# Four modulations of the second layer computed on VectorE, and a longer weight window

## The chip, the core and the metric

The kernel runs on one core of one Trainium2 chip. The metric is the device time of one execution in microseconds (us), as a median over runs. The engines of the core are TensorE (PE: matrix products), VectorE (DVE), ScalarE (ACT), GpSimd (POOL) and SyncE (SP), which here only issues transfers from HBM.

## What is computed

Two stacked blocks work on 256 tokens of width 1024. The first block has two layers, each of this form; the second block (a scan, two attentions, three gated branches) is not touched.

```python
c_act = jax.nn.silu(c)
for l in range(DEPTH):
    mod = c_act @ w_ada[l] + b_ada[l]
    sh1, sc1, g1, sh2, sc2, g2 = [t[:, None, :] for t in jnp.split(mod, N_ADA, axis=-1)]
    h = rmsnorm(x, norm_mix_g[l]) * (1.0 + sc1) + sh1
    z = h @ w_in[l]
    ...
    x = x + g1 * (o @ w_out[l])
    h = rmsnorm(x, norm_mlp_g[l]) * (1.0 + sc2) + sh2
    x = x + g2 * (jnp.square(jax.nn.relu(h @ w_up[l])) @ w_down[l])
```

`mod` does not depend on x. Below, modulation (l, s) is chunk s of layer l: s = 0 to 5 stand for sh1, sc1, g1, sh2, sc2, g2. Each is a product of one row of 1024 with a 1024x1024 matrix.

## The kernel before

**Weights.** Every fp32 weight arrives in tiles `w` of 128x1024 (512 KB), in the order of one list, `e.stream`. `next_w` (L295) asks for the next `AHEAD_W` entries of the list and splits the next `AHEAD_S`. A split tile becomes a high part `wh` (a cast on ScalarE, L290) and a low part `wl` = w - wh (VectorE, L292), and TensorE takes three matmuls for each block of it: high by high, low by high, high by low (`mm`, L318). All tiles share 8 buffers `w` (`NW`) and 4 pairs `wh`, `wl` (`NS`), so a transfer on SP's queue waits until a buffer is read for the last time. Tiles of `w_ada` are used whole, without a split.

**A modulation on TensorE.** `ada_step` multiplies each of the 8 tiles of a modulation with a stationary operand of 32 equal columns (`ca32`, the activated c), 4 blocks a tile, as fp32: the trace counts 64 matmul records for one modulation. `ada_end` copies the sums to SBUF on ScalarE (L515, a buffer of the tag `pt1`, of which there are 2), turns them with 2 small matmuls (`adat`) and adds the bias on VectorE (L520, `mod`).

**A modulation on GpSimd.** `ada_pool` multiplies each tile with a column of c (`tensor_scalar`, L531) and adds it to a running tile of 128x1024 (`tensor_tensor`, L533). `ada_rows` then sums that tile over its partitions on TensorE with ones (4 blocks, 8 records), and `ada_end` follows.

**A norm.** ScalarE squares x in 4 pieces (L406, tag `pt1`), VectorE folds them (L393, L399), TensorE sums over partitions (`st`), VectorE and GpSimd form the inverse root (`rv` L375, `rsy` L358), TensorE spreads it (`bc`), and then for each of 8 chunks VectorE makes `nt` (L551), ScalarE `ah` (L552) and VectorE `al` (L553). The wide products `g` read `ah` and `al`.

**The MLP.** For g = 0 to 15 the product with w_up of group g gives `g`, its squared relu is split into `uh`, `ul` (L970, L971), and one step later the product with w_down of group g is added to four `acc` banks. At the end x += g2 * acc (L1029). Layer 0's MLP is followed by the layer boundary: the norm of layer 1 and its first product, w_in1.

**Where layer 1's modulations stand.** (1,0) and (1,1) on GpSimd during layer 0's MLP (`ad_mlp`), (1,2) and (1,3) on TensorE at the layer boundary (`ad_next`), (1,4) on TensorE at layer 1's second norm (`ad_norm`), (1,5) on GpSimd during layer 1's MLP. Pieces of work wait in one queue, `e.q`; `fill` takes the oldest piece and `need(tag)` empties the queue up to the last piece of a tag. A scheduler then sets each engine's final order from data dependences and priorities; the splits and norms have a raised priority.

## Time and profile before

| | |
|---|---|
| three runs | 1837.41, 1836.98 and 1834.9 us, median 1836.98 us |
| profiled execution | 1838.83 us, of which 1837.0 us are the span |
| mean granted TensorE clock | 0.992 of full speed |
| busy over the span | PE 98%, DVE 73%, ACT 55%, POOL 20% |
| transfers | 346.88 MB, mean 189 GB/s |

Busy means that an instruction runs on the engine; the span is the stretch from the first to the last instruction. Idle time of an engine is noted with what ended it, which is an inference from semaphores.

### The profile page before, as it was taken

What the parts mean: (1) busy time and instruction counts of PE and PEld (TensorE: products, weight loads), DVE (VectorE), ACT (ScalarE), POOL (GpSimd) and SP (SyncE); (2) the same over time, 40 slices, a digit from 0 to 9 for tenths busy, and PEclk for the clock granted to TensorE, in tenths of its full rate; (3) what the DMA queues carried; (4) which work ended last, traced back from release to release, by engine and by line L of the source; (5) the groups of instructions that cost most, each with busy time, mean ns of one, the idle gap of its engine ahead of it and who ended that gap; (6) DMA issues with size and microseconds to landing.
All of it is one profiled execution on the core that took longest, in us unless ns stands there. A gap on an engine that the chain in (4) does not pass through costs nothing.

```text
span 1837.0 us, 37186 instructions
## 1 busy us (share of the span) xinstructions
PE 1791.6 (98%) x14800; PEld 1696.7 (92%) x14800; DVE 1334.8 (73%) x2212; ACT 1017.1 (55%) x1882; POOL 358.9 (20%) x291
## 2 busy tenths in 40 slices
PE   7999999999998999999999999999999999999998
PEld 6878799987878999999999999999999999999998
DVE  4575775756778655798897897566687897997566
ACT  4354444444545444557777575454556687675552
POOL 0000271800007300002444202200001445202200
PEclk9999999999998999999999999999999999999999
DMA  9873886757447655554444644465553445554451
GB/s 335 317 246 129 301 272 197 258 197 294 130 138 282 230 182 183 168 171 140 143 162 154 191 161 148 166 205 175 193 175 130 148 160 162 181 166 168 153 183 60
DMA packets 98223, 346.88 MB, mean 189 GB/s; under 512 B 12288, under 2 KB 13440, under 8 KB 97792
## 3 DMA queue, kind: packets, MB, share of 16 engines
q1 hardware_dynamic: 98048, 344.50, 55.5%
q8 instruction: 116, 1.90, 0.4%
q14 instruction: 59, 0.48, 0.1%
HBM read 339.01 MB, written 1.05 MB: 185 GB/s over the span
## 4 chain that ended last, share of the span: by engine, by line
PE 90%; DVE 3%; ACT 2%; DMA 2%; issue 1%; POOL 0%; POOLq 0%; SPq 0%; DVEq 0%; ACTq 0%
PE g L318 68%; PE acc L318 10%; PE yps L318 2%; DVE wl L292 1%; PE sc L318 1%; PE ada L318 1%; PE ds L318 1%; PE o L318 1%; DMA w<-w_ada 1%; ACT wh L290 1%; PE do L318 1%; PE xs L318 1%; PE xo L318 1%; DMA w<-w_up 1%; PE tw L1153 1%
## 5 line engine op out<-in xcount | busy, mean ns | idle before, releaser
L292 DVE TENSOR_TENSOR wl<-w,wh 128x1024 fp32r<-128x1024 f32 x518 | 664.3, 1285 | 337.7 <-ACT wh L290 335.5
L290 ACT CAST wh<-w 128x1024 fp32r<-128x1024 f32 x518 | 540.6, 1047 | 510.9 <-PE g L318 328.3
L318 PE MATMUL g<-xh,wh 128*128 128x256 f32 x1664 | 477.1, 287 | 0.7 <-DVE cv L1234 0.4
L318 PE MATMUL g<-xl,wh 128*128 128x256 f32 x1664 | 472.3, 284 | 0.0
L318 PE MATMUL g<-xh,wl 128*128 128x256 f32 x1664 | 471.7, 284 | 0.0
L318 PEld LDWEIGHTS g<-xh,wh 128*128 128x128 f32 x1664 | 319.3, 192 | 13.0 <-issue 6.9
L318 PEld LDWEIGHTS g<-xl,wh 128*128 128x128 f32 x1664 | 319.4, 192 | 0.8 <-issue 0.7
L318 PEld LDWEIGHTS g<-xh,wl 128*128 128x128 f32 x1664 | 319.4, 192 | 0.1
L318 PE MATMUL g<-ah,wh 128*128 128x256 f32 x736 | 210.4, 288 | 4.2 <-ACT ah L552 4.2
L318 PE MATMUL g<-al,wh 128*128 128x256 f32 x736 | 210.6, 287 | 2.5 <-DVE al L553 2.5
L318 PE MATMUL g<-ah,wl 128*128 128x256 f32 x736 | 210.8, 287 | 0.7 <-DVE wl L292 0.7
L358 POOL TENSOR_TENSOR rsy<-rv,mhalf 128x2 f32<-128x2 f32 (+1 forms) x14 | 13.4, 958 | 938.8 <-DVE rv L375 831.1
L318 PE MATMUL acc<-pt,wh 128*128 128x256 f32 x1024 | 183.1, 280 | 0.0
L1452 POOL PARTITION_BROADCAST E<-rows x64 | 96.6, 1571 | 389.0 <-PE tw L1153 157.7
L1451 ACT ACTIVATE E<-E,ltok 128x128 f32<-128x128 f32 x384 | 124.5, 394 | 61.9 <-POOL E L1452 57.9
L318 PEld LDWEIGHTS acc<-pt,wh 128*128 128x128 f32 x1024 | 156.8, 188 | 0.4 <-issue 0.4
L318 PEld LDWEIGHTS g<-ah,wh 128*128 128x128 f32 x736 | 142.2, 194 | 8.0 <-ACT ah L552 4.4
L318 PEld LDWEIGHTS g<-al,wh 128*128 128x128 f32 x736 | 142.7, 194 | 4.5 <-DVE al L553 3.5
L318 PEld LDWEIGHTS g<-ah,wl 128*128 128x128 f32 x736 | 142.6, 194 | 1.3 <-DVE wl L292 1.1
L318 PE MATMUL acc<-pt,wl 128*128 128x256 f32 x512 | 142.3, 279 | 0.0
L531 POOL TENSOR_SCALAR sb<-w,ca 128x1024 f32<-128x1024 f32 x24 | 89.3, 3721 | 62.6 <-PE ada L318 32.8
L318 PEld LDWEIGHTS acc<-pt,wl 128*128 128x128 f32 x512 | 96.2, 188 | 0.0
(384 smaller groups left out, 3571.4 us busy)
## 6 DMA issues: line engine op xcount, KB each, us to landing
w<-w_ada SPq DMA_DIRECT2D x96, 512.0 KB
w<-w_up SPq DMA_DIRECT2D x64, 512.0 KB
w<-w_down SPq DMA_DIRECT2D x64, 512.0 KB
w<-w_br SPq DMA_DIRECT2D x64, 512.0 KB
w<-w_gl SPq DMA_DIRECT2D x48, 512.0 KB
w<-w_in SPq DMA_DIRECT2D x36, 512.0 KB
w<-w_mem SPq DMA_DIRECT2D x32, 512.0 KB
w<-w_out SPq DMA_DIRECT2D x32, 512.0 KB
```

The lines of the kernel that those rows point to most:

```text
L290: nc.scalar.copy(wh, w)
L292: nc.vector.tensor_tensor(wl, w, wh.bitcast(F32), ALU.subtract)
L318: self.nc.tensor.matmul(o, l, r, start=start, stop=stop)
L358: self.nc.gpsimd.tensor_tensor(y, v, self.mhalf[:, 0:cols], ALU.pow)
L531: nc.gpsimd.tensor_scalar(dst, w, ca[:, 2 * n + i : 2 * n + i + 1], None, ALU.mult)
L1153: nc.tensor.transpose(tps[:, kt * S + t * P : kt * S + (t + 1) * P], src[:, t, kt * P : (kt + 1) * P], e.ident)
L1451: ex = lambda o, s, r: nc.scalar.activation(o, o, AF.Exp, bias=bias[:, s, r : r + 1])
L1452: nc.gpsimd.partition_broadcast(E, state["rows"][32 * (h % 4) : 32 * (h % 4) + 1, :])
```

## The change

Modulations (1,0) to (1,3) are computed by VectorE during layer 0's MLP (`ada_vec`): the first tile by a `tensor_scalar`, each of the next seven by a `scalar_tensor_tensor` that multiplies and adds to the running sum. Two modulations share one buffer `rows` of 128x2048 taken from a pool that exists already. The key of number j (of 16, two tiles each) is placed at g = 1 + 7j // 8. After the last tile, `ada_rows` is put at the end of the queue. (1,4) alone stays on TensorE at the boundary, (1,5) goes to TensorE at layer 1's second norm, and GpSimd has no modulation. `AHEAD_W` is 12 instead of 8, with 8 buffers as before; whole tiles count as ready as soon as they are asked for. In the list of tiles, w_up of group 1 stands ahead of the modulation of the second norm, and the second tile pair of w_in1 of layer 1 ahead of that of the boundary.

```diff
@@ -204,7 +204,8 @@
 
 
 NW, NS = 8, 4
-AHEAD_W, AHEAD_S = 8, 4
+AHEAD_S = 4
+AHEAD_W = NW + AHEAD_S
 SPLIT_FIRST, NORM_FIRST = 100, 200
 NU = 11
 ALPHA = (2 * DEPTH) ** 0.25
@@ -279,10 +280,13 @@
             ent[2] = self.t(self.wp, [P, 1024], "w", bufs=NW)
             self.last_dma = self.nc.sync.dma_start(ent[2], ap[:, i * 1024 : (i + 1) * 1024])
 
+    def _whole(self, ent):
+        return ent[0][0].startswith(("w_ada", "cmp_"))
+
     def _split(self, ent):
         nc = self.nc
         key, _, w, _ = ent
-        if key[0].startswith(("w_ada", "cmp_")):
+        if self._whole(ent):
             ent[3] = w
             return
         with self.tc.high_priority(offset=SPLIT_FIRST):
@@ -295,7 +299,7 @@
     def next_w(self, *key):
         for i, ent in enumerate(self.wq[:AHEAD_W]):
             self._fetch(ent)
-            if i < AHEAD_S and ent[3] is None:
+            if ent[3] is None and (i < AHEAD_S or self._whole(ent)):
                 self._split(ent)
         i = next(i for i, ent in enumerate(self.wq) if ent[0] == key)
         assert self.wq[i][3] is not None, key
@@ -458,10 +462,16 @@
 
     ad_early = lambda l: ada(l, 2) if l == 0 else []
     ad_mix = lambda l: ada(l, 3) + ada(l, 4) if l == 0 else []
-    ad_norm = lambda l: ada(l,5) if l == 0 else ada(l,4)
-    ad_mlp = lambda l: [(1,0),(1,1)] if l == 0 else [(1,5)]
-    ad_next = lambda l: ada(l+1,2)+ada(l+1,3)
-    mlp_keys = lambda l: {1 + 6 * i + n: [("w_ada", *p, n)] for i, p in enumerate(ad_mlp(l)) for n in range(4)}
+    ad_norm = lambda l: ada(l, 5)
+    ad_mlp = lambda l: [k for s in range(4) for k in ada(1, s)] if l == 0 else []
+    ad_next = lambda l: ada(l + 1, 4)
+
+    def mlp_keys(l):
+        out = {}
+        for j, key in enumerate(ad_mlp(l)):
+            out.setdefault(1 + 7 * j // 8, []).append(key)
+        return out
+
     MEM = 6
     a0 = ada(0, 0) + ada(0, 1)
     start = [[], a0[0:2], a0[2:4], a0[4:6], a0[6:8], []]
@@ -470,16 +480,17 @@
     for l in range(DEPTH):
         W = lambda i: ("w_in1", l, zorder[i])
         ea, am = ad_early(l), ad_mix(l)
-        e.stream(*([] if l else [W(0)]), W(1), W(2), *ea[0:2], ("cmp_k1", l), W(3), *ea[2:3], ("cmp_v1", l), W(4), *ea[3:4], W(5))
+        e.stream(*([] if l else [W(0), W(1)]), W(2), *ea[0:2], ("cmp_k1", l), W(3), *ea[2:3], ("cmp_v1", l), W(4), *ea[3:4], W(5))
         e.stream(W(6), *am[0:2], ("w_out1", l, 0), *am[2:3], W(7), ("w_out1", l, 1), *am[3:4], W(8), *am[4:])
-        e.stream(("w_out1", l, 2), ("w_out1", l, 3), ("w_up", l, 0), *ad_norm(l))
+        e.stream(("w_out1", l, 2), ("w_out1", l, 3), ("w_up", l, 0), ("w_up", l, 1), *ad_norm(l))
         nxt = mlp_keys(l)
         for g in range(16):
+            if g > 1:
+                e.stream(("w_up", l, g))
             if g >= 1:
-                e.stream(("w_up", l, g))
                 e.stream(("w_down", l, g - 1))
             e.stream(*nxt.get(g, []))
-        e.stream(("w_down", l, 15), *([("w_in1", l + 1, zorder[0])] if l + 1 < DEPTH else []), *ad_next(l))
+        e.stream(("w_down", l, 15), *([("w_in1", l + 1, zorder[i]) for i in range(2)] if l + 1 < DEPTH else []), *ad_next(l))
     e.stream(*[("w2_mem", 0, k) for k in range(MEM, 8)])
 
 
@@ -519,18 +530,21 @@
             v = lambda tl, i0: tl[:, i0 : i0 + 8].rearrange("p (j c) -> p c j", j=4)
             nc.vector.tensor_tensor(v(mods[l], s * 8), v3(tp[:, 0:8], 2), v(b_ada, l * 48 + s * 8), ALU.add)
 
-    def ada_pool(l, s, n):
+    def ada_vec(l, s, n):
 
         if n == 0:
-            boxes[l, s] = e.t(ap_, [P, 1536], "sb", bufs=2)[:, 0:D]
+            if s % 2 == 0:
+                boxes["rows"] = e.unit("rows")
+            boxes[l, s] = boxes["rows"][:, s % 2 * D : (s % 2 + 1) * D]
         rows = boxes[l, s]
         for i in range(2):
-            w = e.next_w("w_ada", l, s, n)
-            first = n == 0 and i == 0
-            dst = rows if first else e.t(ap_, [P, 1536], "sb", bufs=2)[:, 0:D]
-            nc.gpsimd.tensor_scalar(dst, w, ca[:, 2 * n + i : 2 * n + i + 1], None, ALU.mult)
-            if not first:
-                nc.gpsimd.tensor_tensor(rows, rows, dst, ALU.add)
+            w, c = e.next_w("w_ada", l, s, n), ca[:, 2 * n + i : 2 * n + i + 1]
+            if n == 0 and i == 0:
+                nc.vector.tensor_scalar(rows, w, c, None, ALU.mult)
+            else:
+                nc.vector.scalar_tensor_tensor(rows, w, c, rows, ALU.mult, ALU.add)
+        if n == 3:
+            e.add("mlp", lambda: ada_rows(l, s))
 
     def ada_rows(l, s):
         ps = e.gbank("ada")
@@ -539,7 +553,7 @@
 
     def ada_add(tag, keys):
         for key in keys:
-            e.add(tag, lambda key=key: (ada_pool if tag == "mlp" else ada_step)(*key[1:]))
+            e.add(tag, lambda key=key: (ada_vec if tag == "mlp" else ada_step)(*key[1:]))
 
     def norm_stats(src):
         return e.rms_wide(ap_, src, 1e-6)
@@ -1020,9 +1034,6 @@
             if g == 16:
                 e.add("mlp", lambda: down_last(15))
             ada_add("mlp", steps.get(g, []))
-            for i, p in enumerate(ad_mlp(l)):
-                if g == 6 * i + 8:
-                    e.add("mlp", lambda p=p: ada_rows(*p))
         e.need("mlp")
         ada_add("next", ad_next(l))
         for k in range(KC):
```

Three places in the engines' orders follow. In the rows of the changed kernel the line numbers are its own: L296 is `wl`, L526 the copy and L531 the `mod` of `ada_end`, L543 and L545 the operations of `ada_vec`, L565 to L567 the norm's `nt`, `ah`, `al`.

**VectorE at the second norm of layer 0.** `wl` of 128x1024 is the low part of w_up, group 1. Before:

```order
L292 TENSOR_TENSOR wl_2369<-w_2343,wh_2367 128x1024
L551 SCALAR_TENSOR_TENSOR nt_2385<-x_370,A_415_2383,bc_2321 128x256
L551 SCALAR_TENSOR_TENSOR nt_2389<-x_370,A_415_2383,bc_2321 128x256
L292 TENSOR_TENSOR wl_2424<-w_2349,wh_2422 128x1024
L520 TENSOR_TENSOR mod_13_105<-adat_2379,pack_1_70 128x2x4
L553 SCALAR_TENSOR_TENSOR al_2300<-nt_2385,mod_13_105,ah_2299 128x256
L553 SCALAR_TENSOR_TENSOR al_2300<-nt_2389,mod_13_105,ah_2299 128x256
L551 SCALAR_TENSOR_TENSOR nt_2393<-x_370,A_415_2383,bc_2321 128x256
L551 SCALAR_TENSOR_TENSOR nt_2397<-x_370,A_415_2383,bc_2321 128x256
L553 SCALAR_TENSOR_TENSOR al_2300<-nt_2393,mod_13_105,ah_2299 128x256
L553 SCALAR_TENSOR_TENSOR al_2300<-nt_2397,mod_13_105,ah_2299 128x256
```

After, from the fourth `nt` of the same norm on (`rows` is the running sum of modulation (1,0)):

```order
L565 SCALAR_TENSOR_TENSOR nt_2409<-x_378,A_421_2395,bc_2333 128x256
L543 TENSOR_SCALAR rows_2611<-w_2359,ca_98 128x1024
L567 SCALAR_TENSOR_TENSOR al_2312<-nt_2405,mod_13_105,ah_2311 128x256
L567 SCALAR_TENSOR_TENSOR al_2312<-nt_2409,mod_13_105,ah_2311 128x256
L565 SCALAR_TENSOR_TENSOR nt_2413<-x_378,A_421_2395,bc_2333 128x256
L545 SCALAR_TENSOR_TENSOR rows_2611<-w_2365,ca_98,rows_2611 128x1024
L565 SCALAR_TENSOR_TENSOR nt_2417<-x_378,A_421_2395,bc_2333 128x256
L567 SCALAR_TENSOR_TENSOR al_2312<-nt_2413,mod_13_105,ah_2311 128x256
L545 SCALAR_TENSOR_TENSOR rows_2611<-w_2371,ca_98,rows_2611 128x1024
L565 SCALAR_TENSOR_TENSOR nt_2421<-x_378,A_421_2395,bc_2333 128x256
L567 SCALAR_TENSOR_TENSOR al_2312<-nt_2417,mod_13_105,ah_2311 128x256
L545 SCALAR_TENSOR_TENSOR rows_2611<-w_2377,ca_98,rows_2611 128x1024
```

The two `wl` have moved ahead of the norm, to its first `fold` operations, and four of the new operations stand between `nt` and `al`.

**TensorE and ScalarE at the layer boundary.** TensorE before, where `ada_4584` is modulation (1,2) and `ada_4639` is (1,3):

```order
L318 MATMUL ada_4584<-w_4597,ca_11_101 32x256 x4
L318 MATMUL ada_4639<-w_4603,ca_11_101 32x256 x4
L318 MATMUL st_4574<-ones_72,fold_4565 128x1 x2
L318 MATMUL ada_4639<-w_4609,ca_11_101 32x256 x4
L318 MATMUL bc_4581<-pack_1_70,rsy_4579 128x128 x2
L318 MATMUL adat_4635<-pack_1_70,pt_725_4633 128x4 x2
L318 MATMUL ada_4639<-w_4615,ca_11_101 32x256 x4
L318 MATMUL ada_4639<-w_4621,ca_11_101 32x256 x4
L318 MATMUL g_4749<-ah_4559,wh_4463 128x256
```

TensorE after, from the end of layer 0's MLP on; `ada` read from `rows` are the sums of (1,0) to (1,3), `ada_4638` is (1,4):

```order
L322 MATMUL ada_4559<-rows_2611,ones_12_103 32x256 x3
L322 MATMUL ada_4570<-rows_2611,ones_12_103 32x256 x4
L322 MATMUL ada_4581<-rows_3549,ones_12_103 32x256 x4
L322 MATMUL adat_4566<-pack_1_70,pt_707_4564 128x4 x2
L322 MATMUL ada_4592<-rows_3549,ones_12_103 32x256 x4
L322 MATMUL adat_4577<-pack_1_70,pt_710_4575 128x4 x2
L322 MATMUL ada_4638<-w_4369,ca_11_101 32x256 x4
L322 MATMUL ada_4638<-w_4377,ca_11_101 32x256 x4
L322 MATMUL ada_4638<-w_4407,ca_11_101 32x256 x3
L322 MATMUL adat_4588<-pack_1_70,pt_713_4586 128x4 x2
L322 MATMUL ada_4638<-w_4407,ca_11_101 32x256
```

ScalarE before, where L406 are the squares of the norm:

```order
L290 CAST wh_4493<-w_4371 128x1024
L406 ACTIVATE pt_707_4561<-x_370 128x512
L406 ACTIVATE pt_708_4563<-x_370 128x512
L406 ACTIVATE pt_710_4567<-x_370 128x512
L406 ACTIVATE pt_711_4570<-x_370 128x512
L515 COPY pt_725_4633<-ada_4584 128x256
L552 ACTIVATE ah_4559<-nt_4698,mod_14_106 128x256
```

ScalarE after, where L410 are the same squares:

```order
L294 CAST wh_4511<-w_4332 128x1024
L294 CAST wh_4639<-w_4362 128x1024
L526 COPY pt_707_4564<-ada_4559 128x256
L526 COPY pt_710_4575<-ada_4570 128x256
L526 COPY pt_713_4586<-ada_4581 128x256
L526 COPY pt_716_4597<-ada_4592 128x256
L410 ACTIVATE pt_721_4615<-x_378 128x512
L410 ACTIVATE pt_722_4617<-x_378 128x512
```

One modulation has left TensorE here, the sums of all four have come, and four copies and one more pair of casts stand ahead of the squares.

**VectorE at the second norm of layer 1.** Before, the two `wl` belong to w_up of group 1, and `A` is computed from the modulation that TensorE does here:

```order
L399 TENSOR_TENSOR fold_6190<-fold_6190 128x256
L292 TENSOR_TENSOR wl_6254<-w_6228,wh_6252 128x1024
L375 TENSOR_SCALAR rv_6202<-st_6199 128x2
L292 TENSOR_TENSOR wl_6309<-w_6234,wh_6307 128x1024
L520 TENSOR_TENSOR mod_14_106<-adat_6264,pack_1_70 128x2x4
L958 SCALAR_TENSOR_TENSOR A_1015_6268<-mod_14_106,pack_1_70 128x8
L551 SCALAR_TENSOR_TENSOR nt_6270<-x_370,A_1015_6268,bc_6206 128x256
L551 SCALAR_TENSOR_TENSOR nt_6274<-x_370,A_1015_6268,bc_6206 128x256
```

After:

```order
L963 SCALAR_TENSOR_TENSOR x_378<-g_6168,mod_14_106,x_378 128x256 x2
L296 TENSOR_TENSOR wl_6211<-w_5807,wh_6209 128x1024
L397 TENSOR_TENSOR fold_6189<-fold_6189,pt_999_6191 128x512
L397 TENSOR_TENSOR fold_6189<-fold_6189,pt_1000_6194 128x512
L403 TENSOR_TENSOR fold_6189<-fold_6189 128x256
L379 TENSOR_SCALAR rv_6201<-st_6198 128x2
L565 SCALAR_TENSOR_TENSOR nt_6269<-x_378,A_1018_6267,bc_6205 128x256
L565 SCALAR_TENSOR_TENSOR nt_6273<-x_378,A_1018_6267,bc_6205 128x256
L531 TENSOR_TENSOR mod_14_106<-adat_6263,pack_1_70 128x2x4
```

Both `wl` are ahead of the norm's last folds, and `A` is no longer in this stretch; it is computed at the boundary.

## Rows read from the trace of the kernel before

**Rows 1.** Stretches: length, busy of PE, PEld, DVE, ACT, POOL; PEclk, DMA share, GB/s.

```profile
203.00:241.30 38.30, 34.48 (x293) 31.97 (x292) 28.83 (x41) 17.67 (x27) 24.12 (x9) 0.91 0.78 276
241.30:404.00 162.70, 162.70 (x1370) 160.98 (x1368) 106.36 (x94) 75.41 (x88) 72.63 (x23) 1.00 0.67 224
404.00:431.00 27.00, 24.19 (x249) 18.00 (x247) 15.37 (x31) 10.14 (x18) 0.72 (x1) 1.00 0.95 357
431.00:546.10 115.10, 109.94 (x895) 95.45 (x894) 82.61 (x254) 57.28 (x142) 2.34 (x2) 0.99 0.46 154
546.10:582.00 35.90, 28.04 (x247) 25.98 (x246) 28.07 (x37) 17.28 (x25) 21.03 (x8) 0.86 0.77 271
582.00:746.00 164.00, 164.00 (x1384) 163.45 (x1383) 100.58 (x95) 76.78 (x88) 28.59 (x9) 1.00 0.61 205
746.00:1837.00 1091.00, 1079.90 (x8764) 1042.79 (x8762) 854.92 (x1353) 674.19 (x1310) 206.24 (x234) 1.00 0.49 161
sum 1837.00, PE 1791.63 PEld 1696.71 DVE 1334.81 ACT 1017.09 POOL 358.89; mean PE 223.95 PEld 212.09 DVE 166.85 ACT 127.14 POOL 44.86
```

**Rows 2.** Timeline of PE: start, duration, [idle before, what ended it]; second norm, layer 0.

```profile
205.63 3.66 PE L318 MATMUL ada<-w,ca 128*32 128x256 f32 x64
210.93 0.71 PE L318 MATMUL bc<-pack,rsy 128*128 128x128 f32 x4 [1.10 <-POOL rsy L358]
213.79 0.50 PE L318 MATMUL g<-ah,wh 128*128 128x256 f32 x2 [1.31 <-ACT ah L552]
```

**Rows 3.** Timeline of DVE, the same place.

```profile
212.72 0.87 DVE L551 SCALAR_TENSOR_TENSOR nt<-x,A,bc 128x256 f32<-128x256 f32 x2
216.56 1.62 DVE L553 SCALAR_TENSOR_TENSOR al<-nt,mod,ah 128x256 fp32r<-128x256 f32 x2 [0.19 <-ACT ah L552]
221.86 0.89 DVE L553 SCALAR_TENSOR_TENSOR al<-nt,mod,ah 128x256 fp32r<-128x256 f32 x2 [0.18 <-ACT ah L552]
```

**Rows 4.** Line L1182: duration ns min/median/max of a 128x1024 operation on two tensors.

```profile
L1182 DVE SCALAR_TENSOR_TENSOR r<-r,mv,gb x2: 1274/1275/1276, 1826.0 to 1831.0; 128x1024 f32<-128x1024 f32 x2
```

**Rows 5.** Timeline of PE in layer 0's MLP: sums of one modulation, and its turn.

```profile
385.06 0.64 PE L318 MATMUL ada<-sb,ones 128*32 128x256 f32 x8
388.83 0.50 PE L318 MATMUL adat<-pack,pt 128*128 128x4 f32 x4
```

**Rows 6.** Timelines of PE and DVE at the layer boundary.

```profile
404.06 3.65 PE L318 MATMUL ada<-w,ca 128*32 128x256 f32 x62
414.14 0.39 PE L318 MATMUL g<-ah,wh 128*128 128x256 f32 x1
420.90 0.64 PE L318 MATMUL ada<-w,ca 128*32 128x256 f32 x8
411.83 0.87 DVE L551 SCALAR_TENSOR_TENSOR nt<-x,A,bc 128x256 f32<-128x256 f32 x2 [1.60 <-PE bc L318]
430.78 0.69 DVE L687 COPY z<-g 128x512 f32<-128x512 f32 x1 [2.46 <-PE g L318]
```

**Rows 7.** Timeline of PE, second norm of layer 1.

```profile
546.15 3.66 PE L318 MATMUL ada<-w,ca 128*32 128x256 f32 x64
554.39 1.22 PE L318 MATMUL bc<-pack,rsy 128*128 128x128 f32 x4 [4.04 <-POOL rsy L358]
559.15 0.80 PE L318 MATMUL g<-ah,wh 128*128 128x256 f32 x2 [2.90 <-ACT ah L552]
```

**Rows 8.** Timelines of ACT, DVE and POOL, the same place.

```profile
551.18 1.04 ACT L290 CAST wh<-w 128x1024 fp32r<-128x1024 f32 x1 [3.14 <-DMA w<-w_up]
552.26 1.23 DVE L292 TENSOR_TENSOR wl<-w,wh 128x1024 fp32r<-128x1024 f32 x1 [3.03 <-ACT wh L290]
556.54 1.23 DVE L292 TENSOR_TENSOR wl<-w,wh 128x1024 fp32r<-128x1024 f32 x1 [2.98 <-ACT wh L290]
565.48 3.01 DVE L553 SCALAR_TENSOR_TENSOR al<-nt,mod,ah 128x256 fp32r<-128x256 f32 x2 [0.18 <-ACT ah L552]
565.65 2.56 POOL L533 TENSOR_TENSOR sb<-sb,sb 128x1024 f32<-128x1024 f32 x1
```

## The prediction

> **What bounds the kernel now.** I read the stretches first [rows 1]. TensorE is busy 1791.63 of 1837.0 us, so nothing that only relieves another engine helps unless TensorE was waiting for it. In the two MLPs (241.3 to 404, 582 to 746) TensorE is busy in all of the 162.70 and 164.00 us: 1370 matmuls in 162.70 us are one each 0.119 us. There a wide matmul is the price of everything, and VectorE (106.36 us) has slack. The idle time that this change can reach lies in three short stretches: the second norm of layer 0 (34.48 busy of 38.30), the layer boundary (24.19 of 27.00) and the second norm of layer 1 (28.04 of 35.90). In the two norms the granted clock is also below 1 (0.91 and 0.86), meaning that for part of the stretch it stood at the lower of its levels, 1.2 instead of 2.4 GHz; the shortfall is worth 0.09 x 38.3 = 3.4 us and 0.14 x 35.9 = 5.0 us. At the boundary it is 1.00. Block 2 (746 to the end) keeps its instructions in the same order.
>
> Next I asked the timelines who is late there. In layer 1's second norm TensorE waits 4.04 us for the inverse root (bc <- rsy) and 2.90 us for the first ah [rows 7]. Neither is slow in itself: VectorE stood at `wl` of the next w_up tile for 3.03 and then 2.98 us, because ScalarE's cast waited 3.14 us for that tile's transfer [rows 8]. The root and the first nt are queued behind those two `wl`. Layer 0 has the same norm with waits of 1.10 and 1.31 us [rows 2]. Beside GpSimd's modulation an `al` pair takes 3.01 and 1.62 us where 0.89 is normal [rows 3, 8].
>
> **The change, part by part.** Terms are against the profiled execution, 1838.83 us.
>
> (a) *Second norm of layer 1.* The w_up tiles of group 1 now stand ahead of the 8 modulation tiles in SP's queue, so their `wl` come before the folds and nothing of the norm is behind a transfer. The modulation made here is (1,5), used only at the end of the MLP, so nt needs no fresh `A`. GpSimd is silent. The like-for-like model is layer 0: first wide product 213.79 - 205.63 = 8.2 us after the modulation's start [rows 2]. From there the 168 wide matmuls of this stretch take 168 x 0.119 = 20.0 us, together 28.2 us, and 31.6 us if the clock falls as in layer 0 (3.4 us). Before it is 582.0 - 546.15 = 35.85 us. So -7.7 to -4.3. The dear bound is layer 0 as it is: 241.3 - 205.63 = 35.7 us for 192, less 24 x 0.119 = 32.8 us, or -3.0. TensorE still idles before the first product, as layer 0's clock row shows it can't do unpunished: I take **-4.2**, range -6 to -3. What could be late next is the modulation's own tiles, now 4 places later in the queue: 4 x 512 KB at 271 GB/s [rows 1] are 7.7 us of transfer, but they are not needed by the norm.
>
> (b) *Sums of GpSimd's modulations.* Three groups of `ada_rows` leave the insides of the MLPs, where TensorE has no idle time to hide them: 0.64 + 0.50 us [rows 5], less about 0.1 each because a matmul's record (0.39 in [rows 6]) overlaps the start of the next: 0.95 each. Two in layer 0, one in layer 1: **-2.85**. The four new groups all come behind the last w_down, into (d), but for one of 16 blocks that sits inside the last `acc` run and breaks it: **+0.4**, taken from one turn with its gap.
>
> (c) *VectorE in layer 0's MLP.* 32 operations of 128x1024. The trace has none of this kind on this operand, the nearest row is a scalar_tensor_tensor of the same shape at 1.275 us [rows 4]; GpSimd's 2.56 for its add [rows 8] is the far bound. 32 x 1.275 = 40.8, so VectorE is busy 106.4 + 40.8 = 147 of 162.7 us: hidden over the MLP as a whole. Not at its start: four of them and the two `wl` of w_down 0 stand inside the nt, al chain of layer 0's second norm. The chain ended at 221.86 + 0.89 = 222.75 [rows 3]. It starts 1.0 us sooner (212.72 no longer behind a `wl`), loses GpSimd's surcharge (0.7 + 0.85), and gains 4 x 1.275 + 2 x 1.23 = 7.6: about 227.8. TensorE meanwhile has the 96 matmuls of groups 0 and 1 (11.4 us, and 3.4 for the clock) from about 213, so it reaches 228 by itself. Behind that, `wl` of group 2 and the split of the relu now follow two further modulation operations and two `wl` (2.55 + 2.46, to 232.8), while 48 matmuls of either kind last 5.7 us. TensorE waits between nothing and 232.8 - 228.8 = 4.0 us; since half of the next work is there in time I take **+1.3**, range -1.5 (the start gained, nothing waited for) to +4.
>
> (d) *Layer boundary.* Before: from 404.06 to the end of the second w_in1 product, about 430.6 (z at 430.78), 26.5 us [rows 6]. It held two modulations, 128 records; the second one's stood in the norm's idle time or between the wide products (420.90 the last). After: 30 records of sums and 64 of (1,4) at 3.65 / 62 = 0.059 us [rows 6] are 5.5 us, turns and `st` about 2.4, so the statistics are ready at 7.9 us after the MLP's end. From a modulation's end to nt layer 0 takes 212.72 - 209.29 = 3.4 us [rows 2, 3]; nt at 11.3, or 12.7 because ScalarE's squares now stand behind four copies that share two buffers and wait for TensorE's turns in between. Before, nt began 411.83 - 404.06 = 7.8. Then 1.1 us to the first product (213.79 - 212.72) and 96 matmuls, 11.4 us: 23.8 to 25.3 us if the clock stays, up to 28.7 us if it falls. That is -2.7 to +2.2. The old boundary kept a full clock [rows 1], but it filled the norm's gap with modulation tiles; the new one has only `bc` and one turn in it. I lean to the dear side: **+0.6**.
>
> The clock's row says that it fell in the gaps at 205 to 215 and not in this one. The Trainium skill (TensorE: Matmul & The Clock Gate, "What's actually happening") states that the clock follows how busy the engine has been of late. By that rule the emptier gap loses the 3.4 us, and (d) would be +2.2; by the row, which is of the filled gap, it would be -1.2. No row here shows the emptied gap.
>
> (e) *Mixers of layer 1.* TensorE idles 115.1 - 109.9 = 5.2 us there [rows 1]; the order of wide products among the small transposes of its second half is changed, the products are the same. **-0.5**, -2 to +1.
>
> (f) *Longer window, nothing gained by itself.* SP already stands at a transfer until one of 8 buffers is free; 12 entries in the list ask earlier, but the buffers are still 8. What moves is the list's order, costed in (a) and (c). At the start some small constants come behind four more tiles, long before their use: 0 (±0.3). No transfer bounds an MLP: the 16 tiles of two more modulations in layer 0's add 8.4 MB to 162.7 us at 224 GB/s, +52 GB/s, against 357 reached at the boundary [rows 1].
>
> Sum: -4.2 - 2.85 + 0.4 + 1.3 + 0.6 - 0.5 = -5.25, so 1833.6 us for an execution like the profiled one. That one was 1.85 us above the median of the runs shown; against the median the forecast is 1836.98 - 5.25 = 1831.7, say **1832**.
>
> **Rivals.** *The gain is eaten at the two places in front* (c at +4, d at +2.2): -5.25 + 2.7 + 1.6 = -0.95, or -2.5 with one of them; 1834.5 to 1836. For it: both norm chains visibly get longer. Against: TensorE has other work at (c).
>
> *VectorE becomes the bound of layer 0's MLP.* Its place is the new operations, its price the slope above the point (162.7 - 106.4) / 32 = 1.76 us an operation. At the far bound, 2.56, VectorE needs 188 us, 26 more than the MLP lasts, and the kernel ends at about 1858; at 2.1 us the 11 us more leave it at 1843. For it: the only figure for this very product on whole tiles is GpSimd's. Against: VectorE does the same shape in 1.275 [rows 4] with GpSimd silent. A smaller way to the same side, at +4 for each norm with the clock lost twice, ends near 1840.
>
> The Trainium skill (SBUF — State Buffer, "SBUF: two separate sides") calls the port pair of VectorE and GpSimd an exclusive lock for the whole instruction. By that an `al` beside GpSimd's 2.56 us add would lose up to 2.56 us; the pair in [rows 8] lost 2.1 and that of [rows 3] 0.7, so the lock holds in part, and by the full rule (a) would be about 1 us better.
>
> *The gain is larger*: no clock loss in either (a) or (d), (e) at -2: -5.25 - 3.4 - 1.8 - 1.5 = about -12, 1825.
>
> *The reordering doesn't reach the waits*: buffers come free late, w_up 1 still arrives after the norm's statistics in layer 1, (a) is -1 for the silent GpSimd alone; the sum is -2 and the time 1835. Against it: four tiles ahead of the eight is the whole order of one queue.
>
> **How the numbers follow.** The forecast's own range, -3.7 to -8.5, gets 0.53; the larger gain 0.06; gain eaten, 0.20; waits not reached, 0.09; slower by VectorE or by two late norms, 0.12. A median of this kernel can tell about 0.2% (3.7 us) from no change, so faster is 0.53 + 0.06 = 0.59, within 0.2% 0.20 + 0.09 = 0.29, slower 0.12. The range leaves out the slower case and most of the large gain: 1826 to 1838.
>
> **What would show it.** (a): PE's wait for rsy in layer 1's second norm near 1 us instead of 4.04, no cast waiting for w_up, first g about 8 us after the modulation's start, the stretch to the 168th product near 31.6. (b): no `ada` record inside the MLPs, and 162.7 and 164.0 shorter by 1.9 and 0.95. (c): `rows` operations near 1.28 us; above 1.76 the forecast is wrong and the MLP longer. (d): nt 11 to 13 us after the last acc; a granted clock under 1 there means the dear end. If block 2's 1091 us move by over 1 us, something I have not seen is at work.

## The result: slower by 0.9 %, where 0.3 % faster was forecast

The changed kernel takes 1854.73 us (median of 4 runs, 1852.52 to 1856.44), the kernel before 1837.2 us beside it. The ratio on record is 1.0087, 95% interval 1.0071 to 1.0104 (the two medians alone give 1.0095). The forecast was 1832 us with a range up to 1838. The profiled execution of the changed kernel took 1854.42 us, its span is 1852.6 us.

The page of the changed kernel, the span and part 1 (busy us, share of the span):

```profile
span 1852.6 us, 37053 instructions
PE 1801.2 (97%) x14744; PEld 1704.4 (92%) x14744; DVE 1330.4 (72%) x2244; ACT 1017.1 (55%) x1882; POOL 210.9 (11%) x246
```

VectorE got 32 operations more and is busy for 4 us less than before (1334.81 in [rows 1]); already this speaks against the load. Next the stretches, cut at the same points of the work as those of [rows 1], from the second norm of layer 0 to block 2, with the same columns:

```profile
203.40:243.70 40.30, 35.08 (x293) 31.56 (x292) 32.72 (x50) 18.03 (x28) 0.69 (x1) 0.92 0.86 297
243.70:417.70 174.00, 167.37 (x1346) 164.87 (x1344) 112.57 (x114) 73.48 (x83) 0.00 (x0) 0.97 0.74 249
417.70:448.00 30.30, 26.56 (x226) 22.32 (x225) 18.25 (x37) 13.32 (x25) 0.69 (x1) 0.83 0.69 249
448.00:565.30 117.30, 113.41 (x898) 97.56 (x896) 80.92 (x251) 56.81 (x142) 1.49 (x2) 0.97 0.40 131
565.30:600.40 35.10, 29.63 (x247) 26.38 (x246) 24.11 (x40) 16.44 (x24) 0.69 (x1) 0.85 0.72 258
600.40:763.20 162.80, 162.80 (x1371) 162.80 (x1371) 89.79 (x91) 76.53 (x87) 0.00 (x0) 1.00 0.57 186
763.20:1852.60 1089.40, 1078.28 (x8764) 1041.36 (x8762) 853.77 (x1353) 673.90 (x1310) 204.16 (x234) 1.00 0.49 161
```

Read the lengths against [rows 1]: +2.0, **+11.3**, **+3.3**, +2.2, -0.8, -1.2, -1.6 us. Layer 0's MLP, where TensorE had never idled, now has 6.6 us without a matmul and a granted clock of 0.97. The clock is not what makes it long: the run win8 below has the same order on TensorE, VectorE, ScalarE and GpSimd, a granted clock of 1.00 in this stretch and 10.7 us without a matmul, and the stretch is as long:

```profile
250.18:424.76 174.58, 163.92 (x1347) 160.53 (x1346) 112.11 (x114) 73.43 (x83) 0.00 (x0) 1.00 0.73 248
```

The boundary is 3.3 us longer and has lost its full clock (0.83).

Who is late in the MLP, the waits of VectorE in that stretch (us in total, times, longest):

```profile
DVE rows L545 <- DMA w<-w_ada: 36.0, 10, 5.4
DVE rows L543 <- DMA w<-w_ada: 12.0, 3, 5.9
DVE wl L296 <- ACT wh L294: 11.7, 11, 1.7
```

VectorE stands 48 us at tiles of w_ada. With 112.6 us of work and 60 us of waits it is taken for 172 of 174 us. One group of the MLP in the timelines of VectorE and of SP's queue shows how:

```profile
267.47 1.22 DVE L296 TENSOR_TENSOR wl<-w,wh 128x1024 fp32r<-128x1024 f32 x1
268.63 0.69 DVE L984 TENSOR_TENSOR pt<-pt,g 128x512 f32<-128x512 f32 x1
274.76 1.28 DVE L545 SCALAR_TENSOR_TENSOR rows<-w,ca,rows 128x1024 f32<-128x1024 f32 x1 [5.43 <-DMA w<-w_ada]
275.96 0.68 DVE L985 TENSOR_TENSOR pt<-pt,pt 128x512 fp32r<-128x512 f32 x1
276.56 1.22 DVE L296 TENSOR_TENSOR wl<-w,wh 128x1024 fp32r<-128x1024 f32 x1
278.89 3.49 DVE L296 TENSOR_TENSOR wl<-w,wh 128x1024 fp32r<-128x1024 f32 x3
```

```profile
262.25 2.06 SPq L281 DMA_DIRECT2D w<-w_up  x2
265.19 1.46 SPq L281 DMA_DIRECT2D w<-w_down  x2
267.46 1.59 SPq L281 DMA_DIRECT2D w<-w_ada  x2
276.07 2.06 SPq L281 DMA_DIRECT2D w<-w_up  x2
```

SP asks for two tiles of w_up, two of w_down and then two of w_ada. VectorE's next instruction reads a tile of w_ada, so it waits for a transfer asked for after the four others. Behind it stand `pt` (the low half of the squared relu, L985) and the `wl` of those four tiles. And SP asks for nothing from about 269 to 276.07: by the trace its next transfer waits until that same operation has released a buffer (276.05), and the five behind it wait for a `wl`, the second operation and three more `wl`. It is a ring: the last tile asked for is the first one VectorE wants, and no further tile is asked for until it has it.

### The profile page after: what moved, and what is told of

Same layout as the page of the kernel before. It is cut to its first block, busy times and chain, and to the rows that moved or that the text cites. A ratio compares the mean times of both kernels' runs of the same rounds, so it can differ in the third digit from the quotient of the medians.

```text
span 1852.6 us, 37053 instructions
## 1 busy us (share of the span) xinstructions
PE 1801.2 (97%) x14744; PEld 1704.4 (92%) x14744; DVE 1330.4 (72%) x2244; ACT 1017.1 (55%) x1882; POOL 210.9 (11%) x246
## 4 chain that ended last, share of the span: by engine, by line
PE 89%; DVE 4%; DMA 3%; ACT 2%; issue 1%; POOLq 0%; POOL 0%; SPq 0%; DVEq 0%; ACTq 0%
PE g L322 67%; PE acc L322 9%; DMA w<-w_ada 2%; DVE wl L296 2%; PE yps L322 1%; PE sc L322 1%; PE o L322 1%; PE ada L322 1%; PE ds L322 1%; PE do L322 1%; PE xo L322 1%; PE xs L322 1%; ACT wh L294 1%; PE tp L666 1%; PE tw L1164 1%
## 5 line engine op out<-in xcount | busy, mean ns | idle before, releaser
L296 DVE TENSOR_TENSOR wl<-w,wh 128x1024 fp32r<-128x1024 f32 x518 | 639.1, 1239 | 297.4 <-ACT wh L294 293.5
L322 PE MATMUL acc<-pt,wh 128*128 128x256 f32 x1024 | 188.6, 284 | 1.9 <-DVE pt L985 1.9
L322 PEld LDWEIGHTS acc<-pt,wh 128*128 128x128 f32 x1024 | 160.9, 192 | 3.0 <-DVE pt L985 2.6
L1245 DVE SCALAR_TENSOR_TENSOR cv<-g,pack,cv 128x254 f32<-128x254 f32 (+1 forms) x192 | 90.2, 477 | 2.3
```

What stands on the lines that cost most here:

```text
L296: nc.vector.tensor_tensor(wl, w, wh.bitcast(F32), ALU.subtract)
L322: self.nc.tensor.matmul(o, l, r, start=start, stop=stop)
L1245: nc.vector.scalar_tensor_tensor(a_[:, a:b], p_[:, a + j - 2 : b + j - 2], conv_w[:, i0 + j : i0 + j + 1], a_[:, a:b], ALU.mult, ALU.add)
```

## The experiments

For each run the trace was cut into stretches by the work done, by TensorE's records: from layer 0's second modulation at the norm, (0,5), to the 49th `acc` matmul (norm 0), to the last `acc` (MLP 0), to the 96th wide product behind it (boundary), to layer 1's second norm (mixers), to its 49th `acc` (norm 1), to its last `acc` (MLP 1), to the end (block 2). Each cut lies at the start of an instruction. Lengths in us, of one profiled execution each; the ratios are those of the timed runs against the kernel before on the same chip.

| run | norm 0 | MLP 0 | boundary | mixers | norm 1 | MLP 1 | block 2 | ratio (95% interval) |
|---|---|---|---|---|---|---|---|---|
| before | 35.5 | 162.8 | 26.5 | 115.8 | 38.7 | 161.1 | 1091.1 | |
| changed | 37.5 | 174.1 | 29.8 | 118.1 | 37.8 | 159.9 | 1089.6 | 1.0087 (1.0071 to 1.0104) |
| resident | 36.5 | 166.2 | 28.8 | 117.8 | 37.7 | 159.9 | 1089.6 | 1.0014 (0.9999 to 1.0028) |
| pin2 | 36.9 | 160.4 | 29.8 | 116.8 | 40.5 | 159.9 | 1091.1 | 1.0011 (1.0000 to 1.0023) |
| early | 38.0 | 173.3 | 26.1 | 115.3 | 38.0 | 159.9 | 1090.7 | 1.0068 (1.0049 to 1.0087) |
| stream | 35.8 | 162.8 | 31.0 | 117.2 | 41.1 | 161.1 | 1091.0 | 1.0043 (1.0026 to 1.0060) |
| pinold | 35.0 | 160.4 | 33.1 | 116.8 | 35.1 | 159.9 | 1090.1 | 1.0000 (0.9985 to 1.0015) |
| best | 36.8 | 160.4 | 31.8 | 120.1* | 29.7* | 160.4 | 1099.3 | 1.0027 (1.0018 to 1.0036) |
| win8 | 37.0 | 174.6 | 29.8 | 118.1 | 38.1 | 159.9 | 1090.2 | 1.0108 (1.0084 to 1.0132) |
| tag | 35.8 | 160.4 | 27.6 | 116.3 | 35.1 | 159.9 | 1089.0 | 0.9951 (0.9935 to 0.9967) |
| early2 | 35.3 | 165.1 | 26.3 | 116.7 | 36.8 | 159.9 | 1091.5 | 0.9977 (0.9962 to 0.9993) |
| best4 | 35.6 | 160.4 | 26.0 | 123.3* | 29.3* | 161.1 | 1095.2 | 0.9950 (0.9931 to 0.9968) |
| tagnew | 35.9 | 160.4 | 24.1 | 113.6 | 39.1 | 159.9 | 1091.0 | 0.9936 (0.9921 to 0.9951) |
| tag8 | 35.0 | 160.4 | 26.0 | 117.6 | 36.7 | 159.9 | 1090.4 | 0.9941 (0.9925 to 0.9958) |

*These two have no modulation at layer 1's second norm; the mark is the first `st`, so only the sum of the two columns compares with the others.* What lies before norm 0 is 203 to 207 us in all but win8, and differs by 1 to 3 us between executions with the same order there; single stretches outside the MLPs should be read with that in mind: tag and tag8, which have one order on these four engines, differ by up to 1.6 us in a stretch. Of block 2 the same holds, but for the two runs discussed. In early, pin2, pinold, best and early2 a group of 8 small `st` matmuls, 1.0 us, stands just ahead of the cut at the boundary's end; in the others at most 4 of the 8 do (before, stream), and the rest counts to the mixers.

**resident: the wait taken away, the transfers kept.**

```diff
             w, c = e.next_w("w_ada", l, s, n), ca[:, 2 * n + i : 2 * n + i + 1]
+            w = flat(x[:, 0:4, :])
```

(and each operation held behind the instruction that it followed in the changed kernel, or one nearby)

> The changed kernel, but VectorE's 32 new operations read a tile of x that has long been in SBUF instead of the tile of w_ada (so modulations (1,0) to (1,3) are not computed); all transfers stay, and the operations are pinned close to the places they had. Theory A, the wait: VectorE takes its instructions in order and stands 48 us at tiles of w_ada, with splits of tiles that landed earlier queued behind. Then without the wait layer 0's MLP (174.1 us from the 192nd wide matmul) goes back to 162 to 165 us and the run to 1840 to 1845 us. Theory B, the load: 32 operations are too much for VectorE; then nothing changes, 1853 to 1856 us. Theory C, the transfers: eight buffers can't bring six tiles per group of the MLP in time; then the casts of ScalarE wait instead, and the run stays above 1850 us.

Theory A holds, theory B falls: 32 operations on VectorE without the wait cost 0.14 %, not 0.87 %. The MLP shrinks by 7.8 us. 3.5 us over the old length stay, and 3.8 us without a matmul on TensorE (162.51 busy of 166.30), at a granted clock of 1.00. They are of theory C's kind: TensorE waits for `wl` and casts, `wl` for casts, and these for transfers, as the waits of ScalarE and of SP's queue in that stretch show:

```profile
ACT wh L294 <- DMA w<-w_up: 51.7, 14, 6.8
SPq L281 <- DMA w<-w_ada: 107.9, 24, 9.8
```

The casts wait for tiles of w_up, which in the changed kernel they never did, and SP's queue stands at tiles of w_ada until they have landed; no instruction reads those tiles in this run. So resident exchanges one wait for a smaller one; the next run keeps the readers.

**pin2: the order of the transfers kept on VectorE.**

```diff
+            self.wls[key] = nc.vector.tensor_tensor(wl, w, wh.bitcast(F32), ALU.subtract).ins
...
+            with tc.issue_after(after()):
                 if n == 0 and i == 0:
...
+                e.add("mlp", lambda key=key, g=g, l=l: ada_vec(*key[1:], lambda: e.wls["w_down", l, g - 1]))
```

> The changed kernel with one constraint more: on VectorE the new operations of group g may not stand ahead of the split of w_down of group g-1, that is, they keep the order in which the tiles are fetched. Theory A: the waits for w_ada (48 us) shrink below 10 us, the MLP comes to 162 to 166 us, the second norm of layer 0 loses 2 to 3 us as well since nothing stands in its chain, 1838 to 1844 us. Theory B: 1853 to 1856 us. Theory C: VectorE waits as long at the new place, or ScalarE at its casts; above 1850 us.

MLP 0 falls from 174.1 to 160.4 us, below the 162.8 of before. The stretch in this run, and VectorE's groups in it (count, busy us, mean ns, idle before):

```profile
243.70:404.10 160.40, 160.40 (x1348) 159.86 (x1346) 119.53 (x117) 73.54 (x83) 0.00 (x0) 1.00 0.81 283
```

```profile
L298 DVE TENSOR_TENSOR wl<-w,wh 128x1024 fp32r<-128x1024 f32 x56 | 68.5, 1224 | 38.7 <-ACT wh L296 38.7
L548 DVE SCALAR_TENSOR_TENSOR rows<-w,ca,rows 128x1024 f32<-128x1024 f32 x24 | 30.8, 1282 | 0.4
```

TensorE has no gap, the clock is back at 1.00, and the new operations wait 0.4 us instead of 48. The same tiles come through the same eight buffers, at 283 GB/s instead of 249: theory C falls. What made the MLP long was the order on VectorE: one constraint on it takes 13.7 us off, with the rest of the change in place. But the run as a whole is where the kernel before is, 1.0011; expected were 1838 to 1844 us beside a kernel before at 1837, and 1842.85 came out beside 1840.5. The two MLPs are 3.6 us shorter than before (2.85 forecast), but norm 0, the boundary, the mixers and norm 1 together are 7.5 us longer. So other terms of the forecast are wrong too.

**stream: the list of tiles alone, on the kernel before (and whole tiles ready at once).** Two lines of the edit:

```diff
-        e.stream(("w_out1", l, 2), ("w_out1", l, 3), ("w_up", l, 0), *ad_norm(l))
+        e.stream(("w_out1", l, 2), ("w_out1", l, 3), ("w_up", l, 0), ("w_up", l, 1), *ad_norm(l))
...
-        e.stream(("w_down", l, 15), *([("w_in1", l + 1, zorder[0])] if l + 1 < DEPTH else []), *ad_next(l))
+        e.stream(("w_down", l, 15), *([("w_in1", l + 1, zorder[i]) for i in range(2)] if l + 1 < DEPTH else []), *ad_next(l))
```

> The kernel before, with only the two moves in the list of tiles (w_up 1 ahead of the second norm's modulation, the second w_in1 pair ahead of the boundary's) and whole tiles ready at once; window 8, modulations where they were. The prediction's step (a) says that the casts' wait for w_up in layer 1's second norm (3.14 and 2.96 us) and TensorE's wait for the root (4.04 us) go, and the stretch from the modulation's start to the 168th product falls from 35.9 to below 33 us: the run is 2 to 4 us faster than before. The rival: the modulation's own eight tiles now land later, TensorE stands at them with the statistics queued behind, and the stretch stays at 35 us: no change.

Neither forecast came: it is slower by 0.43 %. Norm 1 grows by 2.4 us, the boundary by 4.5. TensorE at layer 1's second norm in this run:

```profile
553.27 3.13 PE L318 MATMUL ada<-w,ca 128*32 128x256 f32 x48
558.78 1.08 PE L318 MATMUL ada<-w,ca 128*32 128x256 f32 x8 [2.39 <-DMA w<-w_ada]
561.60 1.08 PE L318 MATMUL ada<-w,ca 128*32 128x256 f32 x8 [1.74 <-DMA w<-w_ada]
562.61 1.01 PE L318 MATMUL st<-ones,fold 128*128 128x1 f32 x4
```

The casts' wait for w_up is gone as forecast, and the rival's wait has come in its place: the modulation's last tiles are four places later in the list, TensorE stands at them, and `st`, on which the whole norm hangs, stands behind. The modulation that took 3.66 us [rows 7] takes 9.3.

**early: the sums of the modulations inside the MLP.**

```diff
-            e.add("mlp", lambda: ada_rows(l, s))
+            e.q.insert(0, ("mlp", lambda: ada_rows(l, s)))
```

> The changed kernel, but the sums over partitions of each of the four modulations are queued right behind its last tile instead of behind the MLP. If the layer boundary (30.2 us from the MLP's end to the 96th wide product, 26.5 before) is long because four sums, copies and turns stand ahead of the norm, it falls to 24 to 26 us, the MLP gets up to 4 us longer, and the run is 1 to 4 us faster than the changed kernel. If it is long because the tiles of (1,4) come late, the boundary stays at 29 to 30 us and the run is the same or up to 4 us slower.

The boundary falls by 3.6 us to 26.1; the late tiles of (1,4) are not what makes it long. The MLP is no longer for it, since TensorE has gaps there to put the sums in (4.9 us without a matmul are left of 6.6). In early2, where it has none, the same edit makes MLP 0 4.7 us longer.

**pinold and tag: the boundary.** pinold is pin2 with the list of the kernel before. tag is pinold with one more edit:

```diff
-            row = e.t(ap_, [P, 512], "pt1", bufs=2)[:, 0:S]
+            row = e.t(ap_, [P, S], "nt", bufs=2)
```

> The pinned kernel (new operations behind the splits of w_down g-1) with the list of tiles as in the kernel before: w_up 1 behind the second norm's modulation, the second w_in1 pair behind the boundary's. Theory D, the list's two moves cost by themselves: they delay the tiles of a modulation that TensorE takes ahead of the norm's statistics. Then the boundary falls from 29.8 to 25 to 27 us, the second norm of layer 1 from 40.5 to 36 to 39 us, that of layer 0 to 35 to 36 us, and the run is 4 to 7 us below the pinned kernel, 1834 to 1838 us, at or below the kernel before. If the boundary is long because of the four sums and copies, it stays at 29 us or more and the run within 2 us of the pinned kernel.

> As pinold, but the copy of a modulation's sums takes a buffer of the tag nt (free at that time) instead of one of the two pt1 buffers that the norm's squares use. Theory E: at the boundary of pinold (33.1 us) the squares stand behind four copies, each of which waits until TensorE has turned the one before, so the statistics are late (TensorE waits 4.7 us for the last fold) and VectorE's splits come in between. Then the boundary falls by 5 to 8 us to 25 to 28 us, all else stays, and the run is 5 to 8 us faster than pinold, 0.2 to 0.4 % faster than the kernel before. Rival: the four sums themselves and the tiles of (1,4) on TensorE set the length; the boundary stays at 31 us or more.

pinold did half of what was expected: norm 1 falls from 40.5 to 35.1 us, norm 0 by 1.8, but the boundary rises to 33.1 and the run stays at 1.0000. Why, ScalarE at pinold's boundary shows; the MLP's last `acc` starts at 400.1:

```profile
402.48 0.37 ACT L527 COPY pt<-ada 128x256 f32<-128x256 f32 x1 [0.63 <-PE adat L324]
403.59 0.37 ACT L527 COPY pt<-ada 128x256 f32<-128x256 f32 x1 [0.74 <-PE adat L324]
405.54 0.63 ACT L412 ACTIVATE pt<-x 128x512 f32<-128x512 f32 x1 [1.59 <-PE adat L324]
407.06 0.63 ACT L412 ACTIVATE pt<-x 128x512 f32<-128x512 f32 x1 [0.89 <-PE adat L324]
408.35 1.04 ACT L296 CAST wh<-w 128x1024 fp32r<-128x1024 f32 x1 [0.66 <-DMA w<-w_in]
409.31 1.14 ACT L412 ACTIVATE pt<-x 128x512 f32<-128x512 f32 x2
```

The squares (L412) wait for `adat`: squares and copies share two buffers, and a buffer is free when TensorE has turned the copy in it. In between a cast waits for w_in1. TensorE meanwhile stood at the statistics:

```profile
413.58 0.86 PE L324 MATMUL st<-ones,fold 128*128 128x1 f32 x4 [4.74 <-DVE fold L405]
```

In tag, with a buffer of another tag for the copies, the squares run at once and `st` overtakes half of modulation (1,4), which then fills the norm's gap:

```profile
400.25 0.63 ACT L412 ACTIVATE pt<-x 128x512 f32<-128x512 f32 x1
401.03 0.64 ACT L412 ACTIVATE pt<-x 128x512 f32<-128x512 f32 x1
405.78 0.58 PE L324 MATMUL st<-ones,fold 128*128 128x1 f32 x4
406.29 1.93 PE L324 MATMUL ada<-w,ca 128*32 128x256 f32 x32
```

`st` comes 6.7 us after the start of the MLP's last `acc` (399.1) instead of 13.4. The boundary is 27.6 us, and the run 1830.22 us, a ratio of 0.9951. Theory E, the buffers shared by squares and copies, holds for the boundary: it is 5.5 us shorter than in pinold, 4.5 of them without the `st` group. Between the two ratios lie about 9 us; the edit reaches the copies of all modulations, and where the other 4 us come from the trace doesn't show beyond the differences of 1 to 2 us named above.

**early2, best, best4: where the sums go.** early2 is pinold with the edit of early. best is pinold with (1,5) on VectorE in layer 1's MLP, best4 the same on tag with the sums of (1,5) inside the MLP.

> As pinold, but the sums of each modulation are queued right behind its last tile, inside the MLP. By theory E the boundary falls to 25 to 27 us as it did in the run early, while the MLP, which has no idle time on TensorE, gets four groups of sums of 0.95 us back: 160.4 becomes 164 us. Net 2 to 4 us faster than pinold, so slower than the run tag by about the price of the groups that the boundary hides.

> As pinold, and modulation (1,5) leaves TensorE and layer 1's second norm: VectorE computes it in layer 1's MLP, one key at each of the groups 2, 4, 6 and 8, pinned in the same way. If TensorE's own modulation ahead of the statistics is what holds the second norm of layer 1, that stretch (38.7 us before, 37.8 in the changed kernel) falls to 31 to 34 us, the MLP behind it stays at 160 to 162 us, and the run is 4 to 7 us faster than pinold and 0.2 to 0.6 % faster than the kernel before. If the norm's chain itself (squares, folds, root) is what holds it, the stretch stays above 36 us.

> As tag, and (1,5) on VectorE in layer 1's MLP with its sums inside the MLP (at the end they held up block 2 by 8 us in the run best, it seems). If that reading of the run best is right, block 2 is back at 1090 to 1091 us, mixers and second norm of layer 1 together stay at 150 us (154.5 before), the MLP behind at 161 to 162, and the run is 0 to 2 us faster than tag. If block 2 stays at 1099 us, the reading is wrong and something else of VectorE's modulation reaches there.

early2 came as expected: boundary 26.3, MLP 165.1, between pinold and tag. best took 4.7 us off mixers and norm 1 together against before (149.8 against 154.5, up to 1.0 of it the place of the `st` group), only 2.1 against pinold (151.9), so not what was expected, and block 2 is 9.2 us longer than in pinold, 7.2 of them lost by its 25th us. There `st` of the last norm waits where before it didn't:

```profile
759.06 0.79 PE L324 MATMUL st<-ones,fold 128*128 128x1 f32 x4 [3.70 <-DVE fold L405]
```

The sums of (1,5), queued behind the MLP (742.60) and turned only at 747.21 behind wide products, hold up the update of x on which that norm rests. With the sums inside the MLP (best4) that wait is not in the trace and block 2 is at 1095.2 us, still 4 over the others; mixers and norm 1 take 152.6. So the place of the sums was about half the matter, and best4's other 4 us stay open. It is no faster than tag.

**win8 and tag8: the window; tagnew: the list once more.**

```diff
-AHEAD_W = NW + AHEAD_S
+AHEAD_W = NW
```

> The changed kernel with the window of 8 entries instead of 12. The prediction says that the window does nothing since there are 8 buffers: VectorE's, ScalarE's and TensorE's orders are the same instruction by instruction, only a few transfers of constants change places; every stretch within 1 us of the changed kernel's, 1852 to 1856 us. If asking earlier is what brings the tiles of w_ada into the way, VectorE's 48 us of waiting shrink and the run is below 1848 us.

> As tag, with a window of 8 entries instead of 12. Every engine but SP has the same order instruction by instruction; on SP some transfers at the start of each layer change places. The prediction says that the window is worth nothing: every stretch behind the first modulation of layer 0's second norm within 1 us of tag's and the median within 0.2 % of it. If the window is worth something it is in the first 205 us, where the run win8 had lost 7.5 us to the clock; then tag8 is 5 us or more slower than tag.

VectorE, ScalarE, TensorE and GpSimd have the order of the changed kernel in win8 and that of tag in tag8. In win8 all stretches from norm 0 on are within 0.6 us of the changed kernel's; tag8's ratio is 0.9941 against 0.9951. The window is worth nothing that can be measured. Win8's median is above what was expected: of its two runs one took 1856.06 us, the traced one 1862.61. What the traced one lost lies ahead of norm 0, behind a longer wait for a tile of a modulation (2.78 us against 1.40 in the changed kernel). A stretch of win8 there, then the start of one product in win8 and in the changed kernel:

```profile
92.00:107.00 15.00, 15.00 (x56) 7.30 (x59) 4.04 (x5) 5.22 (x7) 0.00 (x0) 0.57 0.42 148
92.11 8.74 PE L322 MATMUL uq<-cqn,w_uq 128*96 128x256 f32 x16
```

```profile
89.97 4.80 PE L322 MATMUL uq<-cqn,w_uq 128*96 128x256 f32 x16
```

From here to the same wide product behind it TensorE takes 15.4 us in win8 (to 107.47) and 9.6 in the changed kernel (to 99.55), in one order, at a granted clock of 0.57 there. Tag8, with the same list in that place, waits for no tile there and has a clock of 1.00.

tagnew is tag with the changed kernel's list, so the changed kernel with two edits, the constraint of pin2 and the buffer of tag:

> As tag, but with the changed kernel's list of tiles (w_up 1 ahead of the second norm's modulation, the second w_in1 pair ahead of the boundary's). If the list's moves cost by delaying the tiles of a modulation that TensorE takes ahead of the statistics, layer 1's second norm goes from 35.1 to 38 to 41 us and the run is 4 to 7 us slower than tag, 1834 to 1837 us; the boundary is to tell whether the move of w_in1 costs there once the copies no longer hold up the squares (27.6 us in tag; 28 to 31 if it does). If the moves cost nothing when nothing else is wrong, it is within 2 us of tag.

Norm 1 is longer by 4.0 us as expected, but the boundary is shorter by 3.5 and the mixers by 2.7: 0.9936, the lowest ratio of all, not the 4 to 7 us above tag that were expected, and not to be told from tag. The move of w_up costs at the norm; the move of w_in1 costs 4.5 us where two modulations follow it (stream) and not where one follows and the squares are free.

## Why the prediction was wrong, step by step

**(c), VectorE in the MLP, +13.2 instead of +1.3** (MLP 0 is 11.3 us longer although (b) takes 1.9 off it). This is the step that failed: it summed the durations of the new operations and put their wait, and that of the splits behind them, at nothing. The price was right: 1.282 us against the 1.275 of [rows 4], and 0.753 for the `tensor_scalar`:

```profile
L545 DVE SCALAR_TENSOR_TENSOR rows<-w,ca,rows x28: 1279/1282/1290, 220.3 to 382.8; 128x1024 f32<-128x1024 f32 x28
L543 DVE TENSOR_SCALAR rows<-w,ca x4: 752/753/754, 218.5 to 340.4; 128x1024 f32<-128x1024 f32 x4
```

The load was no limit: pin2 carries it in full with TensorE busy all the time, and VectorE is busy for 119.5 us there instead of the 147 of the sum (five of the 32 operations lie ahead of the stretch, and other operations became shorter, last section). Left out was the first thing to ask of an instruction put on an in-order engine: what it waits for, and who stands behind it. The prediction had half of it in its own words, that `wl` and the split of the relu "now follow" modulation operations; that these read the tile asked for last it did not ask, and it read them as operations in a norm's chain. Its sign of being wrong, an operation above 1.76 us, never showed, while the MLP grew. Its bound of 4.0 us also subtracts a 228.8 that no step of the sum gives; that moves it by about 1 us. In the kernel before, GpSimd had waited for the first such tile of the second norm of layer 0 too (its timeline there), and no one stood behind it:

```profile
216.39 5.95 POOL L531 TENSOR_SCALAR sb<-w,ca 128x1024 f32<-128x1024 f32 x2 [5.52 <-DMA w<-w_ada]
```

The rival that made VectorE the bound had the right place and the wrong mechanism: its point of 1.76 us an operation is passed only if the wait is counted, 1.22 + 48.0 / 32 = 2.7 us. Its own far bound, 2.56, gave 1858; 1854.7 came; that it lies near is luck, since none of the operations took longer than 1.29 us.

Of the 13.7 us between the changed kernel and pin2 in this stretch, 7.8 go with the wait even at the price of another (resident). In the trace of the changed kernel TensorE has 6.6 us without a matmul, and the lower clock (0.97, an estimate of 0.03 x 174 = 5.2 us) stretches its work; in win8, with the same orders, it has 10.7 us without a matmul, a clock of 1.00 and the same length. So VectorE, taken for 172 of 174 us, sets the length, and what the clock takes is taken from TensorE's waits.

**(d), the boundary, +3.3 (range -2.7 to +2.2).** The mechanism was named, the size was wrong. I let the squares come at most 1.4 us late; they come behind four copies that each wait for a turn, so that the first starts 5.3 us after the MLP's end (0.9 in tag) and `nt` at 432.07, 14.3 us after it where 11.3 to 12.7 stood in the sum, and the clock falls on top (0.83; 0.89 in pin2, whose MLP had a full clock). The row that was missing is there now: the emptied gap lost the clock. Early2, whose gap is emptier still, has 0.81 in the same stretch; tag, in which the modulation fills the gap, 0.94; tagnew, busy for 23.0 of 24.1 us there, 1.00. With this the trace agrees with the rule of the Trainium skill (TensorE: Matmul & The Clock Gate, "What's actually happening") that the clock follows how busy the engine has been of late, and with the dear end that the prediction worked out by it. One reading there was inexact: in the kernel before the clock did not fall in the gaps at 205 to 214 us (granted 1.00) but behind them, from 214.2 to 221.2 (0.51).

**(a), layer 1's second norm, -0.8 instead of -4.2.** The sentence that failed is that the modulation's tiles "are not needed by the norm". By data they aren't; by TensorE's order they are:

```profile
565.39 2.80 PE L322 MATMUL ada<-w,ca 128*32 128x256 f32 x48
571.79 0.96 PE L322 MATMUL ada<-w,ca 128*32 128x256 f32 x8 [3.60 <-DMA w<-w_ada]
574.07 1.01 PE L322 MATMUL st<-ones,fold 128*128 128x1 f32 x4
576.18 1.22 PE L322 MATMUL bc<-pack,rsy 128*128 128x128 f32 x4 [1.10 <-POOL rsy L362]
```

The wait for the root is 1.10 us instead of 4.04, as forecast, and the modulation is 5 us later. With the old list (pinold) the stretch is 35.1, a gain of 3.6, so most of (a) comes without the list's move that was to bring it. What is left to bring it is GpSimd's silence and (1,5) not being needed by the norm; no run separates the two.

**(b), the sums,** right: MLP 1 is 1.2 us shorter (0.95 forecast), MLP 0 of pin2 2.4 (1.9). **(f), the window,** right. **(e), the mixers,** +2.3 instead of -0.5, in no run the same (113.6 to 118.1); not settled. Block 2 is 1.6 us shorter, over the 1 us that was to mean something unseen; tag and tag8, with one order, differ there by 1.4.

## What to carry to other kernels

When work moves to an in-order engine, look at what its operand comes from and at the place of that transfer in the queue: an operation that reads the last tile asked for, ahead of operations that read earlier ones, makes the queue of eight buffers stand still until that tile has landed (7 us in the group shown). The order of the instructions and the list of tiles show that before any run. The work itself was affordable: the changed kernel with two edits (tagnew) is 0.6 % faster than the kernel before. A wait taken out of one place of a shared list (w_up's cast) is put into another (the modulation's tiles), so name who is moved back; and two uses of one small buffer tag are an order between engines that no data asks for: the edit of one line there was worth about 0.5 % of the run (pinold to tag), of which 4.5 to 5.5 us show at the boundary.

## What the hardware showed that was not expected

GpSimd's modulations had cost VectorE more than the two rows of `al` said. In layer 0's MLP a `wl` lasts 1453 ns on average before, 1224 in pin2:

```profile
L292 DVE TENSOR_TENSOR wl<-w,wh 128x1024 fp32r<-128x1024 f32 x56 | 81.1, 1453 | 52.7 <-ACT wh L290 52.6
```

That is 12.8 us over 56 splits, beside 72.8 us of GpSimd; 33 us of added work in that stretch raise VectorE's busy time by 13 only. That GpSimd is the reason shows within the kernel before: the 29 of these splits that no GpSimd instruction overlaps last 1225 ns on average, the 27 that one overlaps 1697. The second step of the relu (`pt`, L971, two operands in SBUF) goes from 693 to 1361 ns in the same way, 6 of 14 overlapped, while the first (L970), which reads `g` in a PSUM bank, stays at 687 and 680.

A wait of TensorE can be followed by a fall of the granted clock, and need not be. At 317 to 323 us of the changed kernel an `acc` matmul waits 1.84 us for a `wl`, and from 319.47 on the pairs of matmuls last 0.63 instead of 0.40 us until 322.67; this happens three times in that MLP, each time behind waits of 1.7 to 1.8 us in all. In win8, waits of 2.17 and 1.51 us in the same MLP were followed by no fall (1.00 over the stretch). What a fall costs depends on who sets the pace: nothing that shows in that MLP, where VectorE does, and 5.8 us ahead of win8's norm 0 (15.4 against 9.6 us), behind a wait of 2.78 us.
